# Where a TensorE operand begins inside its SBUF slot: slots with spare bytes, and a shift that depends on the streaming width

## The chip, the cores and the metric

The kernel runs on one core of one Trainium2 chip. The metric is the device time of one execution in microseconds (us); the time before is the median of three executions. Everything below is float32: the large matrix products run on TensorE (PE) in the type float32r, the rest in float32.

## The reference, cut to what matters

One layer of a hybrid decoder over 512 positions of width 2048. The parts that cost time are the matrix products with the weights w_in, w_glu, w_out, w_gate, w_up and w_down.

```python
h = x
hn = _rmsnorm(h, norm1_g)
q, k, v, u = jnp.split(hn @ w_in, [1024, 2048, 3072], axis=-1)
attn_out = _dilated_attention_mixer(q, k, v, cos, sin)      # 8 heads of 128
ssm_out = _s5_mixer(u, ..., w_glu, b_glu)                   # scan over positions, then GELU and a sigmoid gate
h = h + jnp.concatenate([attn_out, ssm_out], axis=-1) @ w_out
hn = _rmsnorm(h, norm2_g)
h = h + (jax.nn.silu(hn @ w_gate) * (hn @ w_up)) @ w_down   # D_FF = 5632
return _rmsnorm(h, final_g)
```

## The kernel before, in words

All activations are kept transposed: the 128 partitions hold features, the free axis holds the 512 positions. A product tile of 128 output features is summed in one PSUM bank over blocks of 128 input features.

**Three products for one.** To keep float32 accuracy with float32r products, every operand is split into a high part and a low part (`split`: ScalarE, ACT, writes the high part, VectorE, DVE, subtracts it and writes the low part). `mm3` then issues three matmuls for each block: line 108 is high weights times high activations, line 109 high weights times low activations, line 110 low weights times high activations. In each, the weights are the stationary operand (128 columns, loaded by a weight load, PEld), the activations the moving operand that is streamed past it, 512 or 256 columns at a time. In the v product (lines 549 to 551) it is the other way round: the activations x are stationary and the weights are streamed.

**The stages** follow each other on PE in this order: u (the state-space input), q, k and v, each 512 columns wide; attention heads; glu; oa (w_out times the attention half, 512 wide); os (w_out times the state-space half, 256 wide, two passes os0 and os1); gate/up, called gu, 256 wide; dn (w_down, 512 wide); and dl, w_down's last group of four row blocks, 256 wide. Gate and up are computed by a Strassen-like scheme of seven half-width products, A to G, for each of 44 feature tiles and each of the two halves of the input features. In the code's order a half runs A, C, B, D, E, F, G, and each product is four blocks of three matmuls, 12 matmuls. A takes its activations from c1, B also from c1, C from c4, D and F from c3, E and G from c2. The main loop has 11 phases; a phase is four gate/up tiles, and behind the first of them the 16 dn tiles of the phase before. The first five tiles get A and B early, while DVE still makes c2, c3 and c4.

**Where operands lie.** Activations that TensorE streams lie in slots of 4096 bytes per partition (`[128, 2, 512]` of four-byte elements: high half, low half; or two operands of two 256-column halves). The slots are in rings: tag A0 and tag A1 (eight each), B in ring2 (eight), a and C in mlp (four each). A slot is used again and again by whatever has its tag: A0 holds x0 to x7, then the attention outputs attn, then c1; A1 holds x8 to x15, then ssm, then c3; B holds ysp, then c2; a holds the gate/up outputs m; C holds c4. Weights lie in five high and five low buffers of 2048 bytes, used in turn by all products. Small `pad` tiles shift the rings. The allocator's addresses in the built program, as the first byte of an operand within its partition modulo 256 (all parts of an operand lie whole multiples of 256 bytes apart, so one number stands for all):

| operand | streamed in | columns | before | changed |
|---|---|---|---|---|
| x0 to x7 / x8 to x15 | u, q, k (stationary in v) | 512 | 64 / 128 | 0 / 0 |
| ysp | glu | 512 | 192 | 16 |
| attn | oa | 512 | 64 | 32 |
| ssm | os | 256 | 128 | 160 |
| c1 (products A, B) | gate/up | 256 | 64 | 192 |
| c2 (E, G) | gate/up | 256 | 192 | 192 |
| c3 (D, F) | gate/up | 256 | 128 | 192 |
| c4 (C) | gate/up | 256 | 64 | 208 |
| m, phases 1 to 10 | dn | 512 | 0 | 0 |
| m, last phase | dl | 256 | 0 | 192 |
| weights whi, wlo (all stages; streamed in v) | stationary | | 0 | 0 |
| weights whi_dl / wlo_dl, in slots B / A0 | stationary in dl | | 192 / 64 | 0 / 0 |

The order of the work is set by a scheduler when the program is built. It is fixed for each engine; semaphores hold an instruction until what it needs is there. SyncE (SP) issues nearly all DMAs in one queue.

Of the kernel before, what the change touches and what calls it, by code (L numbers as in the profile page):

```python
# [11 lines left out]
F32 = mybir.dt.float32  # L12
F32R = mybir.dt.float32r
# [14 lines left out]
NC_ = 64  # L28
RAW = 4
HB = 5  # L30
EPS = 1e-6
SCALE = HD ** -0.5


def _emit(tc, a, y):
    nc = tc.nc
# [124 lines left out]


    ring = opened("ring", bufs=1)
    pad(ring, 64)
    for t in ("A0", "A1"):
        first = ring.tile([128, 2, 512], F32R, tag=t, name="first" + t, bufs=8)
        nc.gpsimd.memset(first[:, 0, 0:2].bitcast(F32), 0.0)
        if t == "A0":
            pad(ring, 64)

    def slot(tag, name):
        return ring.tile([128, 2, 512], F32R, tag=tag, name=name, bufs=8)

    ssacc = cpool.tile([128, 512], F32, tag="ss", name="ssacc")
    rstd = ssacc
# [120 lines left out]
    for n in (1, 2, 4):  # L296
# [4 lines left out]
        t_ = pt[:, :, :n]  # L301
# [231 lines left out]
    mask = vpool.tile([128, 512], F32, name="mask")  # L533
    nc.sync.dma_start(mask, a["mask"])
    ring2 = opened("ring2", bufs=1, side="right")
    first = ring2.tile([128, 2, 512], F32R, tag="B", name="firstB", bufs=8)
    nc.gpsimd.memset(first[:, 0, 0:2].bitcast(F32), 0.0)
    pad(ring2, 800)


    vs = [vpool.tile([128, 1024], F32, name=f"v{m}") for m in range(4)]
# [15 lines left out]
    for b in range(8):  # L557
        yt = wpool.tile([128, 512], F32, tag="sq", name=f"yt{b}", bufs=4)
        nc.sync.dma_start(yt, sy[b].rearrange("p i c -> p (i c)"))
        t_ = ring2.tile([128, 2, 512], F32R, tag="B", name=f"ysp{b}", bufs=8)  # L560
        split(t_[:, 0, :], t_[:, 1, :], yt)
        ysp.append(t_)

# [20 lines left out]
    for h in range(NH):  # L584
        Pb, Tb = nxt
        if h + 1 < NH:
            nxt = scores(h + 1)
        po = acc(f"po{h}")
        for step in "t0 t1 t2 p0 t3 p1 p2 p3".split():
            j = int(step[1])  # L590
            w = 512 - 128 * j
            PT = Tb[j // 2][:, j % 2, :]
            if step[0] == "t":
                tp = acc(f"tp{h}_{j}")
                for i in range(j, 4):
                    pe.transpose(tp[:, 128 * (i - j):128 * (i - j) + 128], Pb[i // 2][:, i % 2, 128 * j:128 * j + 128], ident)
                act.activation(PT[:, :w], tp[:, :w], AF.Copy)
            else:
                pe.matmul(po[:, 128 * j:512], vs[j][:, 128 * h:128 * h + 128], PT[:, :w], start=j == 0, stop=j == 3)
        o = slot("A0", f"attn{h}")  # L600
        act.activation(o[:, 0, :], po, AF.Copy)
        tt(o[:, 1, :], po, o[:, 0, :].bitcast(F32), ALU.subtract)
        attn.append(o)
# [3 lines left out]
    for f in range(8):  # L607
        ps = acc(f"glu{f}")
        ftile(ps, [a["w_glu"][f]], ysp, f"glu{f}")
        g_ = wpool.tile([128, 512], F32, tag="sq", name=f"gate{f}", bufs=4)  # L610
        act.activation(g_, ps, AF.Sigmoid, bias=bg[:, f:f + 1])
        yt = wpool.tile([128, 512], F32, tag="sq", name=f"yr{f}", bufs=4)
        nc.sync.dma_start(yt, sy[f].rearrange("p i c -> p (i c)"))
        z = wpool.tile([128, NC_, T], F32, tag="sq", name=f"gz{f}", bufs=4)
        tt(z.rearrange("p c i -> p i c"), yt.rearrange("p (i c) -> p i c", i=T), g_.rearrange("p (i c) -> p i c", i=T), ALU.mult)
        o = slot("A1", f"ssm{f}")
        split(o[:, 0, :], o[:, 1, :], z.rearrange("p c i -> p (c i)"))
        ssm.append(o)
    closed("v")
# [14 lines left out]
    ss2 = cpool.tile([128, 512], F32, tag="ss", name="ss2")  # L634
    rstd2 = ss2
    mp = opened("mlp", bufs=1)
    pad(mp, 128)
    first = mp.tile([128, 2, 512], F32R, tag="a", name="firsta", bufs=4)
    nc.gpsimd.memset(first[:, 0, 0:2].bitcast(F32), 0.0)
    pad(mp, 64)  # L640

    def comb(tag, name, pool_=None, bufs=8):

        return (pool_ or ring).tile([128, 2, 2, 256], F32R, tag=tag, name=name, bufs=bufs)

    early = {}

# [6 lines left out]
    def split_early(f, hh):  # L654
        raw = load_first(f, hh)
        early[f, hh] = []
        for i in range(2):
            t_ = ring2.tile([128, 2, 512], F32R, tag="B", name=f"w{'AB'[i]}{f}_{hh}", bufs=8)
            split(t_[:, 0], t_[:, 1], raw[:, 512 * i:512 * i + 512])
            early[f, hh].append((t_[:, 0], t_[:, 1]))  # L660

# [5 lines left out]
    c1, c2, c3, c4, n1 = [], [], [], [], []  # L667

    def first_half(k):
        n_ = mp.tile([128, 2, 2, 256], F32, tag="a", name=f"n1_{k}", bufs=4) if k % 2 == 0 else n1[-1][1]  # L670
        n1.append((n_[:, k % 2], n_))
        tc.keep_in_program_order(norm(n1[k][0][:, 0], k, E[0]))
        norm(n1[k][0][:, 1], k + 8, E[0])
# [60 lines left out]
    def gu(f, bank0=None):  # L734
# [28 lines left out]
        tt(u_[:, E[1]], u_[:, E[0]], P[5], ALU.add)  # L763
        tt(u_[:, E[0]], u_[:, E[0]], P[4], ALU.add)
        tt(g_, g_, u_, ALU.mult)
        o = mp.tile([128, 2, 512], F32R, tag="a", name=f"m{f}", bufs=4)
        split(o[:, 0, :], o[:, 1, :], g_)
        return o

    NEARLY = 5  # L770
    first = [gu_first(f) for f in range(NEARLY)]
    for k in range(8):
        es = E[1]
# [16 lines left out]
        c3.append(t3)  # L790

    ssf = cpool.tile([128, 512], F32, tag="ss", name="ssf")
    NPH = 11

    def down(p, ms):
        for c in range(8):
# [20 lines left out]
    for c in range(8):  # L817
        raw = wpool.tile([128, 1024], F32, tag="raw", name=f"raw_dl{c}", bufs=RAW)
        nc.sync.dma_start(raw, a["w_down"][8 * (NPH - 1) + c])
        hi = ring2.tile([128, 2, 512], F32R, tag="B", name=f"whi_dl{c}", bufs=8).rearrange("p a b -> p (a b)")  # L820
        lo = slot("A0", f"wlo_dl{c}").rearrange("p a b -> p (a b)")
        split(hi, lo, raw)
        ws.append((hi, lo))
# [100 lines left out]
```

## Time and profile before

| | |
|---|---|
| time before, median of 3 executions | 2132.87 us (2131.88 to 2133.87) |
| the profiled execution's own time | 2136.28 us |
| its span, first to last instruction | 2134.5 us |
| PE busy | 2078.9 us (97%), 13522 matmul records |
| PEld busy | 1878.8 us (88%) |
| DVE busy | 1539.8 us (72%) |
| ACT busy | 866.4 us (41%) |
| POOL (GpSimd) busy | 198.2 us (9%) |
| chain that ended last | PE 89%, DVE 6%, the rest 5% |

Busy times are shares of the span. Matmuls are pipelined and their ends are modelled in the profile, so a matmul's recorded duration is longer than the time until the next one starts (a 256-column matmul of gate/up is recorded with about 0.28 us). What PE really spends on a matmul is read from the starts of matmuls that follow each other.

### The profile page before, as it was taken

What the parts mean: (1) busy time and instruction counts of PE and PEld (TensorE: products, weight loads), DVE (VectorE), ACT (ScalarE), POOL (GpSimd) and SP (SyncE); (2) the same over time, 40 slices, a digit from 0 to 9 for tenths busy, and PEclk for the clock granted to TensorE, in tenths of its full rate; (3) what the DMA queues carried; (4) which work ended last, traced back from release to release, by engine and by line L of the source; (5) the groups of instructions that cost most, each with busy time, mean ns of one, the idle gap of its engine ahead of it and who ended that gap; (6) DMA issues with size and microseconds to landing.
All of it is one profiled execution on the core that took longest, in us unless ns stands there. A gap on an engine that the chain in (4) does not pass through costs nothing.

```text
span 2134.5 us, 35169 instructions
## 1 busy us (share of the span) xinstructions
PE 2078.9 (97%) x13522; PEld 1878.8 (88%) x13522; DVE 1539.8 (72%) x2932; ACT 866.4 (41%) x1523; POOL 198.2 (9%) x179
## 2 busy tenths in 40 slices
PE   7899999999999979999999999999999999999996
PEld 5688888877889979899998989899998989999896
DVE  7834897546436889686786858687686868778686
ACT  5222222346325645343443525344352535344354
POOL 4433102300002360000000000000000000000001
PEclk9899999999999989999999999999999999999998
DMA  6444334523325614323232333323232332323232
GB/s 219 125 118 114 96 98 138 163 91 124 123 91 170 205 60 139 119 99 119 96 116 87 106 102 110 115 84 129 89 118 81 110 108 100 119 83 126 89 120 79
DMA packets 117193, 244.24 MB, mean 114 GB/s; under 512 B 39040, under 2 KB 57312, under 8 KB 117024
## 3 DMA queue, kind: packets, MB, share of 16 engines
q1 hardware_dynamic: 107808, 239.88, 34.3%
q10 hardware_dynamic: 9216, 2.10, 0.5%
q8 instruction: 106, 1.74, 0.3%
q14 instruction: 63, 0.52, 0.1%
HBM read 229.77 MB, written 9.03 MB: 112 GB/s over the span
## 4 chain that ended last, share of the span: by engine, by line
PE 89%; DVE 6%; issue 2%; DMA 1%; ACT 1%; POOL 0%; SPq 0%; DVEq 0%; ACTq 0%; POOLq 0%
PE gu L108 13%; PE gu L109 13%; PE gu L110 12%; PE dn L109 7%; PE dn L110 7%; PE dn L108 7%; PE q L109 1%; PE q L110 1%; PE lps L436 1%; PE q L108 1%; PE v L549 1%; PE v L551 1%; PE v L550 1%; PE k L109 1%; PE k L108 1%
## 5 line engine op out<-in xcount | busy, mean ns | idle before, releaser
L109 PE MATMUL dn<-m,whi_dn 128*128 128x512 f32 x640 | 249.0, 389 | 0.0
L110 PE MATMUL dn<-m,wlo_dn 128*128 128x512 f32 x640 | 248.8, 389 | 0.0
L108 PE MATMUL dn<-m,whi_dn 128*128 128x512 f32 x640 | 248.8, 389 | 0.0
L49 DVE TENSOR_TENSOR h<-h,dn 128x512 f32<-128x512 f32 x160 | 110.0, 688 | 172.6 <-PE dn L110 171.5
L89 ACT ACTIVATE whi_dn<-raw_dn 128x512 fp32r<-128x512 f32 x160 | 100.9, 632 | 243.3 <-PE dn L109 208.4
L49 DVE TENSOR_TENSOR raw_r<-raw_r,raw_r 128x512 f32<-128x512 f32 x264 | 183.1, 693 | 2.2
L110 PEld LDWEIGHTS dn<-m,wlo_dn 128*128 128x128 f32 x640 | 120.1, 188 | 24.9
L109 PEld LDWEIGHTS dn<-m,whi_dn 128*128 128x128 f32 x640 | 120.1, 188 | 24.6
L108 PEld LDWEIGHTS dn<-m,whi_dn 128*128 128x128 f32 x640 | 120.1, 188 | 24.6
L49 POOL TENSOR_TENSOR h<-h,ssf 128x256 f32<-128x256 f32 x12 | 10.7, 918 | 1317.2 <-ACT ssf L159 1317.2
L49 DVE TENSOR_TENSOR wlo_dn<-raw_dn,whi_dn 128x512 fp32r<-128x512 f32 x160 | 109.8, 687 | 19.7 <-ACT whi_dn L89 18.4
L108 PE MATMUL gu<-c,whi_D 128*128 128x256 f32 x352 | 99.9, 284 | 2.6 <-ACT whi_D L89 2.6
L110 PE MATMUL gu<-c,wlo_E 128*128 128x256 f32 x352 | 98.8, 281 | 2.6 <-DVE wlo_E L49 2.6
L110 PE MATMUL gu<-c,wlo_D 128*128 128x256 f32 x352 | 99.4, 282 | 2.0 <-DVE wlo_D L49 2.0
L108 PE MATMUL gu<-c,whi_E 128*128 128x256 f32 x352 | 98.7, 280 | 2.3 <-ACT whi_G L89 1.7
L108 PE MATMUL gu<-c,whi_C 128*128 128x256 f32 x352 | 98.8, 281 | 1.7 <-ACT c L89 1.6
L109 PE MATMUL gu<-c,whi_D 128*128 128x256 f32 x352 | 99.9, 284 | 0.0
L109 PE MATMUL gu<-c,whi_F 128*128 128x256 f32 x352 | 99.7, 283 | 0.0
L110 PE MATMUL gu<-c,wlo_F 128*128 128x256 f32 x352 | 99.5, 283 | 0.0
L108 PE MATMUL gu<-c,whi_F 128*128 128x256 f32 x352 | 99.4, 282 | 0.0
L109 PE MATMUL gu<-c,whi_C 128*128 128x256 f32 x352 | 98.9, 281 | 0.1
L110 PE MATMUL gu<-c,wlo_C 128*128 128x256 f32 x352 | 98.5, 280 | 0.5 <-DVE wlo_C L49 0.5
(325 smaller groups left out, 6692.1 us busy)
## 6 DMA issues: line engine op xcount, KB each, us to landing
raw_r<-w_gu SPq DMA_DIRECT2D x176, 512.0 KB, 3.5
raw_dn<-w_down SPq DMA_DIRECT2D x80, 512.0 KB, 3.5
raw_os<-w_out SPq DMA_DIRECT2D x32, 512.0 KB, 3.4
raw_q<-w_q SPq DMA_DIRECT2D x16, 512.0 KB, 3.5
raw_k<-w_k SPq DMA_DIRECT2D x16, 512.0 KB, 3.4
raw_v<-w_v SPq DMA_DIRECT2D x16, 512.0 KB, 3.6
raw_oa<-w_out SPq DMA_DIRECT2D x16, 512.0 KB, 3.5
raw_u<-w_u SPq DMA_DIRECT2D x15, 512.0 KB, 4.9
```

The source lines that it names most:

```text
L49: (eng or dve).tensor_tensor(out=out, in0=in0, in1=in1, op=op)
L89: act.activation(hi, raw, AF.Copy)
L108: pe.matmul(ps, wh, x[:, 0, :], start=first, stop=False)
L109: pe.matmul(ps, wh, x[:, 1, :], start=False, stop=False)
L110: pe.matmul(ps, wl, x[:, 0, :], start=False, stop=last)
L436: pe.matmul(lps[:, g, :], tm_[:, :, :, g].rearrange("p i q -> p (i q)"), U[:, 8 * b + g, :], start=True, stop=True)
L549: pe.matmul(pss[m], xs[kt][:, 0, ms], wh, start=kt == 0, stop=False)
L550: pe.matmul(pss[m], xs[kt][:, 0, ms], wl, start=False, stop=False)
L551: pe.matmul(pss[m], xs[kt][:, 1, ms], wh, start=False, stop=kt == 15)
```

## The change

Each slot grows from 1024 to 1088 elements, 4352 bytes or 17 times 256, so all slots of a ring begin at the same address modulo 256. A new helper `laid` takes 1024 elements out of such a slot from a given element on. The shift is chosen where an operand is made: 0, 4 or 8 elements for those streamed 512 columns at a time, 40, 48 or 52 for those streamed 256 at a time (the table above gives the resulting addresses). The pads and the placeholder tiles `first...` of the rings go, with their memsets; ring2 keeps its own, with another pad. Matmuls, splits and their order on PE, ACT and DVE are the same in both programs.

```diff
--- before.py
+++ after.py
@@ -28,6 +28,7 @@
 NC_ = 64
 RAW = 4
 HB = 5
+RPAD = 992
 EPS = 1e-6
 SCALE = HD ** -0.5
 
@@ -161,15 +162,15 @@
 
 
     ring = opened("ring", bufs=1)
-    pad(ring, 64)
-    for t in ("A0", "A1"):
-        first = ring.tile([128, 2, 512], F32R, tag=t, name="first" + t, bufs=8)
-        nc.gpsimd.memset(first[:, 0, 0:2].bitcast(F32), 0.0)
-        if t == "A0":
-            pad(ring, 64)
-
-    def slot(tag, name):
-        return ring.tile([128, 2, 512], F32R, tag=tag, name=name, bufs=8)
+    SLOT = 1088
+
+    def laid(pool_, tag, name, bufs, o):
+
+        t = pool_.tile([128, SLOT], F32R, tag=tag, name=name, bufs=bufs)
+        return t[:, o:o + 1024].rearrange("p (a b) -> p a b", a=2)
+
+    def slot(tag, name, shift=0):
+        return laid(ring, tag, name, 8, shift)
 
     ssacc = cpool.tile([128, 512], F32, tag="ss", name="ssacc")
     rstd = ssacc
@@ -533,9 +534,9 @@
     mask = vpool.tile([128, 512], F32, name="mask")
     nc.sync.dma_start(mask, a["mask"])
     ring2 = opened("ring2", bufs=1, side="right")
-    first = ring2.tile([128, 2, 512], F32R, tag="B", name="firstB", bufs=8)
+    first = laid(ring2, "B", "firstB", 8, 0)
     nc.gpsimd.memset(first[:, 0, 0:2].bitcast(F32), 0.0)
-    pad(ring2, 800)
+    pad(ring2, RPAD)
 
 
     vs = [vpool.tile([128, 1024], F32, name=f"v{m}") for m in range(4)]
@@ -557,7 +558,7 @@
     for b in range(8):
         yt = wpool.tile([128, 512], F32, tag="sq", name=f"yt{b}", bufs=4)
         nc.sync.dma_start(yt, sy[b].rearrange("p i c -> p (i c)"))
-        t_ = ring2.tile([128, 2, 512], F32R, tag="B", name=f"ysp{b}", bufs=8)
+        t_ = laid(ring2, "B", f"ysp{b}", 8, 4)
         split(t_[:, 0, :], t_[:, 1, :], yt)
         ysp.append(t_)
 
@@ -597,7 +598,7 @@
                 act.activation(PT[:, :w], tp[:, :w], AF.Copy)
             else:
                 pe.matmul(po[:, 128 * j:512], vs[j][:, 128 * h:128 * h + 128], PT[:, :w], start=j == 0, stop=j == 3)
-        o = slot("A0", f"attn{h}")
+        o = slot("A0", f"attn{h}", 8)
         act.activation(o[:, 0, :], po, AF.Copy)
         tt(o[:, 1, :], po, o[:, 0, :].bitcast(F32), ALU.subtract)
         attn.append(o)
@@ -613,7 +614,7 @@
         nc.sync.dma_start(yt, sy[f].rearrange("p i c -> p (i c)"))
         z = wpool.tile([128, NC_, T], F32, tag="sq", name=f"gz{f}", bufs=4)
         tt(z.rearrange("p c i -> p i c"), yt.rearrange("p (i c) -> p i c", i=T), g_.rearrange("p (i c) -> p i c", i=T), ALU.mult)
-        o = slot("A1", f"ssm{f}")
+        o = slot("A1", f"ssm{f}", 40)
         split(o[:, 0, :], o[:, 1, :], z.rearrange("p c i -> p (c i)"))
         ssm.append(o)
     closed("v")
@@ -634,14 +635,10 @@
     ss2 = cpool.tile([128, 512], F32, tag="ss", name="ss2")
     rstd2 = ss2
     mp = opened("mlp", bufs=1)
-    pad(mp, 128)
-    first = mp.tile([128, 2, 512], F32R, tag="a", name="firsta", bufs=4)
-    nc.gpsimd.memset(first[:, 0, 0:2].bitcast(F32), 0.0)
-    pad(mp, 64)
 
     def comb(tag, name, pool_=None, bufs=8):
 
-        return (pool_ or ring).tile([128, 2, 2, 256], F32R, tag=tag, name=name, bufs=bufs)
+        return laid(pool_ or ring, tag, name, bufs, 52 if tag == "C" else 48).rearrange("p a (h t) -> p a h t", h=2)
 
     early = {}
 
@@ -655,7 +652,7 @@
         raw = load_first(f, hh)
         early[f, hh] = []
         for i in range(2):
-            t_ = ring2.tile([128, 2, 512], F32R, tag="B", name=f"w{'AB'[i]}{f}_{hh}", bufs=8)
+            t_ = laid(ring2, "B", f"w{'AB'[i]}{f}_{hh}", 8, 0)
             split(t_[:, 0], t_[:, 1], raw[:, 512 * i:512 * i + 512])
             early[f, hh].append((t_[:, 0], t_[:, 1]))
 
@@ -667,7 +664,7 @@
     c1, c2, c3, c4, n1 = [], [], [], [], []
 
     def first_half(k):
-        n_ = mp.tile([128, 2, 2, 256], F32, tag="a", name=f"n1_{k}", bufs=4) if k % 2 == 0 else n1[-1][1]
+        n_ = laid(mp, "a", f"n1_{k}", 4, 0).bitcast(F32).rearrange("p a (h t) -> p a h t", h=2) if k % 2 == 0 else n1[-1][1]
         n1.append((n_[:, k % 2], n_))
         tc.keep_in_program_order(norm(n1[k][0][:, 0], k, E[0]))
         norm(n1[k][0][:, 1], k + 8, E[0])
@@ -763,11 +760,12 @@
         tt(u_[:, E[1]], u_[:, E[0]], P[5], ALU.add)
         tt(u_[:, E[0]], u_[:, E[0]], P[4], ALU.add)
         tt(g_, g_, u_, ALU.mult)
-        o = mp.tile([128, 2, 512], F32R, tag="a", name=f"m{f}", bufs=4)
+        o = laid(mp, "a", f"m{f}", 4, 48 * (f >= 4 * (NPH - 1)))
         split(o[:, 0, :], o[:, 1, :], g_)
         return o
 
     NEARLY = 5
+    NPH = 11
     first = [gu_first(f) for f in range(NEARLY)]
     for k in range(8):
         es = E[1]
@@ -790,7 +788,6 @@
         c3.append(t3)
 
     ssf = cpool.tile([128, 512], F32, tag="ss", name="ssf")
-    NPH = 11
 
     def down(p, ms):
         for c in range(8):
@@ -817,7 +814,7 @@
     for c in range(8):
         raw = wpool.tile([128, 1024], F32, tag="raw", name=f"raw_dl{c}", bufs=RAW)
         nc.sync.dma_start(raw, a["w_down"][8 * (NPH - 1) + c])
-        hi = ring2.tile([128, 2, 512], F32R, tag="B", name=f"whi_dl{c}", bufs=8).rearrange("p a b -> p (a b)")
+        hi = laid(ring2, "B", f"whi_dl{c}", 8, 0).rearrange("p a b -> p (a b)")
         lo = slot("A0", f"wlo_dl{c}").rearrange("p a b -> p (a b)")
         split(hi, lo, raw)
         ws.append((hi, lo))
```

In the order of the instructions two places differ. On SP the load of `mask` (the attention mask, `[128, 512]`) stood before, between loads for the state-space output (cc, c_c), ahead of the last w_q loads (raw_q):

```order
L94 DMA raw_q_1_2479<-w_q 128x1024
L504 DMA cc_3140<-c_c 128x256
L504 DMA cc_3252<-c_c 128x256
L534 DMA mask<-mask 128x512
L504 DMA cc_3287<-c_c 128x256
L470 DMA sw_q_2284<-qh_2282 16x512
L471 DMA sw_q_2284<-qh_2282 16x512
```

In the changed program it stands among the loads of w_v (raw_v) for the second half of v; behind it come two more of these and the reloads of the state-space output (yt from sy):

```order
L95 DMA raw_v_2_3936<-w_v 128x1024
L95 DMA raw_v_3_3970<-w_v 128x1024
L535 DMA mask<-mask 128x512
L95 DMA raw_v_4_4004<-w_v 128x1024
L95 DMA raw_v_5_4038<-w_v 128x1024
L560 DMA yt_4164<-sy_3452 128x512
```

The load has moved from the middle of the q stage to the v stage. There it waits for the last matmul of the state-space output (yps) and for GpSimd, since its new place overlaps a buffer that they used.

On POOL the start of the program before held the memsets of the pads (line 67) and placeholders (line 167), ahead of the running sum of squares ssacc:

```order
L67 MEMSET pad_58 128x1
L67 MEMSET pad_78 128x1
L167 MEMSET firstA_80 128x2
L67 MEMSET pad_82 128x1
L167 MEMSET firstA_84 128x2
L49 ISA
L49 TENSOR_TENSOR ssacc<-ssacc,sq_x_295 128x512
```

In the changed program one pad is left there:

```order
L917 UNCONDITIONAL_BRANCH
L68 MEMSET pad_58 128x1
L50 ISA
L50 TENSOR_TENSOR ssacc<-ssacc,sq_x_287 128x512
L50 TENSOR_TENSOR ssacc<-ssacc,sq_x_290 128x512
```

Four memsets are gone here, and three more later on.

## Rows read from the trace of the kernel before

**Rows 1.** Busy time by stretch: us, each engine's busy us, PEclk, DMA share, GB/s.

```profile
220.00:370.00 150.00, 150.00 (x676) 123.24 (x676) 129.77 (x393) 35.81 (x57) 17.70 (x12) 1.00 0.36 112
...
692.00:741.00 49.00, 47.76 (x390) 46.58 (x390) 46.12 (x86) 32.34 (x64) 16.97 (x15) 1.00 0.60 199
...
772.00:865.00 93.00, 80.99 (x604) 77.39 (x604) 88.99 (x154) 45.59 (x80) 18.21 (x16) 0.91 0.35 115
865.00:2062.00 1197.00, 1197.00 (x8431) 1122.09 (x8431) 894.05 (x1526) 499.11 (x820) 0.00 (x0) 1.00 0.31 104
2062.00:2134.50 72.50, 53.59 (x442) 51.75 (x440) 51.36 (x114) 33.81 (x77) 10.65 (x12) 0.89 0.28 95
```

**Rows 2.** PE by time, one half of a gate/up tile: start us, recorded us, instruction.

```profile
1671.10 0.28 PE L108 MATMUL gu<-c,whi_A 128*128 128x256 f32 x1
...
1676.76 0.28 PE L108 MATMUL gu<-c,whi_E 128*128 128x256 f32 x1
...
1678.12 0.28 PE L108 MATMUL gu<-c,whi_F 128*128 128x256 f32 x1
...
1679.55 0.28 PE L108 MATMUL gu<-c,whi_G 128*128 128x256 f32 x1
...
1680.93 0.28 PE L108 MATMUL gu<-c,whi_A 128*128 128x256 f32 x1
```

**Rows 3.** Costliest groups of the page, dn: count, busy us, mean ns, idle before.

```profile
L109 PE MATMUL dn<-m,whi_dn 128*128 128x512 f32 x640 | 249.0, 389 | 0.0
```

**Rows 4.** PE by time, one dn tile and the next one's first matmul.

```profile
1364.57 0.39 PE L108 MATMUL dn<-m,whi_dn 128*128 128x512 f32 x1
...
1367.29 0.39 PE L108 MATMUL dn<-m,whi_dn 128*128 128x512 f32 x1
```

**Rows 5.** PE by time, first matmuls of two k tiles that follow each other.

```profile
309.58 0.39 PE L108 MATMUL k<-x,whi_k 128*128 128x512 f32 x1
...
320.65 0.39 PE L108 MATMUL k<-x,whi_k 128*128 128x512 f32 x1
```

**Rows 6.** PE by time, first matmuls of two chunks of v (24 matmuls, x0 to x7).

```profile
436.39 0.40 PE L549 MATMUL v<-whi_v,x 128*128 128x512 f32 x1
...
441.99 0.40 PE L549 MATMUL v<-whi_v,x 128*128 128x512 f32 x1
```

**Rows 7.** PE by time, first matmuls of two glu tiles.

```profile
530.09 0.39 PE L108 MATMUL glu<-ysp,whi_glu 128*128 128x512 f32 x1
...
535.69 0.39 PE L108 MATMUL glu<-ysp,whi_glu 128*128 128x512 f32 x1
```

**Rows 8.** PE by time, first matmuls of two oa tiles.

```profile
585.56 0.39 PE L108 MATMUL oa<-attn,whi_oa 128*128 128x512 f32 x1
...
591.05 0.39 PE L108 MATMUL oa<-attn,whi_oa 128*128 128x512 f32 x1
```

**Rows 9.** PE by time, first matmuls of two os0 tiles.

```profile
660.38 0.28 PE L108 MATMUL os<-ssm,whi_os 128*128 128x256 f32 x1
...
663.26 0.28 PE L108 MATMUL os<-ssm,whi_os 128*128 128x256 f32 x1
```

**Rows 10.** PE by time, 15 dl matmuls.

```profile
2097.22 0.28 PE L108 MATMUL dl<-m,whi_dl 128*128 128x256 f32 x1
...
2099.00 0.28 PE L108 MATMUL dl<-m,whi_dl 128*128 128x256 f32 x1
```

**Rows 11.** PE by time, 12 dl matmuls later on.

```profile
2104.36 0.28 PE L109 MATMUL dl<-m,whi_dl 128*128 128x256 f32 x1
...
2105.72 0.28 PE L109 MATMUL dl<-m,whi_dl 128*128 128x256 f32 x1
```

**Rows 12.** Busy time in a stretch of four gate/up tiles, columns as in rows 1.

```profile
1030.70:1109.50 78.80, 78.80 (x674) 78.79 (x673) 65.50 (x114) 39.76 (x67) 0.00 (x0) 1.00 0.34 114
```

**Rows 13.** Instructions that read the mask: count, ns, first and last start.

```profile
L575 DVE CUSTOM_DVE_ANT_0 P<-sc,mask x32: 280/480/693, 450.6 to 505.3; 128x128 f32<-128x128 f32 x8, 128x256 f32<-128x256 f32 x8, 128x384 f32<-128x384 f32 x8, 128x512 f32<-128x512 f32 x8
```

**Rows 14.** SP by time: the raw_v loads before, and the yt behind them.

```profile
397.90 25.16 SPq L94 DMA_DIRECT2D raw_v<-w_v  x6
423.60 2.13 SPq L559 DMA_DIRECT2D yt<-sy  x4
```

## The prediction

> **What bounds the kernel now.** I read the busy times by stretch first, to find where PE sets the time, then PE's starts inside each stage. From 865 to 2062 us, the regular main loop and 56% of the span, PE is busy all 1197.0 us, with the clock at its upper level (PEclk 1.00, 2.4 GHz), and DVE for 894 us [rows 1]. No wait ends there on another engine, so the time is the number of matmuls times the distance between their starts. Of the 8431 matmuls in it 1920 are dn (three lines of 640), with no idle time before them [rows 3].
>
> A start-to-start distance is the reading that matters. A dn tile of 12 matmuls takes 1367.29 - 1364.57 = 2.72 us, 226.7 ns each [rows 4]. In gate/up, products of the same shape differ: E takes 1678.12 - 1676.76 = 1.36 us for 12, 113.3 ns each; F 1.43 us, 119.2 ns; G 1.38 us, 115 ns; A, C, B and D together 5.66 us for 48, 117.9 ns [rows 2]. The whole half takes 9.83 us for 84, 117.0 ns on average. The stretch agrees: (1197.0 - 1920 x 0.2267) / 6511 = 117.0 ns. E and F have the same weights' buffers in turn, the same shape, no wait; what tells them apart is where the moving operand lies: E's at 192 modulo 256, F's at 128.
>
> Is it the address of the moving operand, or its distance from that of the stationary one? I call (moving - stationary) modulo 256 the **distance**. With 512 columns:
>
> - dn: 0 - 0, distance 0: 226.7 ns [rows 4]
> - oa: 64 - 0, distance 64: 5.49 us for 24, 228.8 ns [rows 8]
> - k: half its matmuls at 64, half at 128: 11.07 us for 48, 230.6 ns [rows 5], so 2 x 230.6 - 228.8 = 232.4 ns at 128
> - glu: 192 - 0, distance 192: 5.60 us for 24, 233.3 ns [rows 7]
> - v: moving weights at 0, stationary x at 64, distance 192: 5.60 us, 233.3 ns [rows 6]
>
> v streams from 0 just as dn does and is not as fast; it has glu's distance and glu's pace. So I read the distance as the cause. With 256 columns: distance 192 is 113.3 ns (E), 128 is 119.2 (F) and 120.0 in os (2.88 us for 24) [rows 2, 9], and 64 is near 117.9 (A, B, C are three of the four products in that sum). dl mixes distances 64, 64 and 192 and runs at two paces: 1.78 us for 15, 118.7 ns, and later 1.36 us for 12, 113.3 ns, with the same distances [rows 10, 11]. So a pace can also be handed on from matmul to matmul. E, behind D at 128, is at 113.3 ns on average at once: 192 draws the stream to the short pace.
>
> **What the change does to each stage.** No matmul, split or DMA of weights is added, removed or reordered on PE, ACT and DVE. Distances become 192 for A, B, D, E, F, G and dl, 208 for C, 160 for os, and 0 for x in u, q, k and (as stationary operand) v; 16 for glu, 32 for oa; dn stays at 0.
>
> - Gate/up in the main loop: 6511 x (117.0 - 113.3) = 24.1 us. I take C at 208 like E's 192, the nearest row, only 16 bytes off; if its 936 matmuls (39 tiles of 24) gained nothing, 4.3 us of this would go.
> - q and k: in the stretch from 220 to 370 us PE is busy throughout with 676 records, 628 of them q and k (three yps groups of 16 are the rest) [rows 1]. 628 x (230.6 - 226.7) = 2.4 us.
> - v: 192 matmuls at 233.3, and 192 at distance 128, for which I take k's 232.4; all to 226.7: 1.3 + 1.1 = 2.4 us.
> - glu: distance 16 lies between 0 (226.7) and 64 (228.8); in proportion 227.2. 192 x 6.1 = 1.2 us, at least 0.9 by the end at 64.
> - oa: 32 is midway, 227.8: 384 x 1.0 = 0.4 us, between 0 and 0.8.
> - os: 160 is midway between 128 (120.0) and 192 (113.3), 116.7. os0: 384 x 3.3 = 1.3 us, between 0 and 2.6. os1: nothing, since there DVE is busy 46.1 of 49.0 us [rows 1]; at most 2.6.
> - From 741 to 865 us nothing: from 772 on DVE, which makes c2, c3 and c4, is busy 89.0 of 93.0 us and PE 81.0, so PE would wait longer. At most 1.5 us (the last three tiles, some 350 matmuls at 117 to 113.3, 1.3 us).
> - dl: a saving of 5.4 ns for the part of 384 matmuls at the longer pace; PE is busy 53.6 of 72.5 us in the tail, with DVE and the last DMAs on the path. I take 0.5 us, between 0 and 1.5.
> - u: nothing, at most 1 us.
> - The mask load: 512 columns, moved past the q, k and first v loads on SP. It now waits for yps, and two raw_v loads and the yt reloads wait behind it. Before, that place of the queue was passed by 423.6 us [rows 14]; the mask is first read at 450.6 us [rows 13]. That leaves 27 us; cost 0. If that cover went, the first scores would wait for it and PE for them, microsecond for microsecond.
> - The seven memsets on POOL: one column or two each, ahead of sums that POOL takes up only when x has arrived; 0.
>
> Sum: 24.1 + 2.4 + 2.4 + 1.2 + 0.4 + 1.3 + 0.5 = 32.3 us. From the profiled execution's 2136.28 us (1.8 us more than its span) that gives 2104.0 us. It stands 3.4 us above the median, so the median becomes 2132.9 - 32.3 = 2100.6, say **2101 us**. With every upper end (oa 0.8, os 5.2, the 1.5 before 865, dl 1.5, u 1.0) the gain is 40 us, 2093. With every lower end (C nothing, os, oa and dl nothing, glu 0.9) it is 25.5 us, 2107.
>
> What hides nothing else: DVE has 65.5 us of recorded work in four gate/up tiles of 78.8 us [rows 12], and these would take 672 x 113.3 = 76.1 us.
>
> A rule that speaks against all this: the Trainium skill (TensorE: Matmul & The Clock Gate, Part 2) gives PE two independent read ports, so that loading the next weights takes no read bandwidth from the running matmul. By it the distance between the two operands cannot matter, and v, dn and glu should run alike; the kernel would stay at 2133. The rows on v and on E against F disagree.
>
> **The rivals.**
>
> 1. *Starts off a multiple of 64 bytes cost.* All streams of the rows lie at multiples of 64; 16, 32, 160 and 208 don't. Bounded by the worst rows (120.0 ns at 256 columns, 233.3 at 512): C at 120.0 costs 936 x 6.7 = 6.3 us against the sum, os gains nothing (1.3), oa loses 384 x 5.5 = 2.1, glu gains nothing (1.2). That is 10.9 us less gain, 2112. For it: no row excludes it. Against it: the paces at 64 and at 128 differ by little. The Trainium skill (SBUF — State Buffer, Specifications) speaks of 16-byte lines; all four starts are multiples of 16, so by that page there is no such cost, and no run here shows it yet.
> 2. *DVE or the split weights come late.* PE is faster by 3%, and gate/up waits for wlo. If half the gain of gate/up is lost, 2113. Against it: 65.5 of 76.1 us [rows 12], and PE never waits in the main loop before.
> 3. *The slot's address is not the cause.* E would be fast for another reason (its weights' place in the order), and nothing moves: 2133, no change. Against it: v, and G, which also reads c2 and starts at 115 ns although F runs ahead of it. (It is the case that the two ports of the Trainium skill's TensorE page, cited above, would give.)
> 4. *Slower: the longer pace is held.* The dl rows show one set of distances at 113.3 and at 118.7. If the whole gate/up stream, now all at 192 and 208, held os's 120.0 ns, the main loop would lose 6511 x 3.0 = 19.5 us against 8.2 us gained elsewhere: 2144. It decides from 117.0 + 8.2 / 6511 = 118.3 ns on. Against it: E falls to 113.3 in every half shown, whatever ran before it.
>
> **How the numbers follow.** My forecast, 0.76: 2093 to 2107, likeliest 2101. Rival 1: 0.10, rival 2: 0.05, rival 3: 0.05, rival 4: 0.04. A change under 0.2% (4.3 us) can't be told from none; only rival 3 lies within it, rivals 1 and 2 are still faster by 0.9%. So faster 0.91, same 0.05, slower 0.04. The range takes in the forecast and most of rival 1: 2092 to 2112.
>
> **What would show it.** In the changed kernel's trace each of the seven products of a half should take 1.36 us from its first start to the next one's, a half 9.52 us; a v chunk 5.44 us; a k tile 10.88 us; dn stays at 2.72. C at 1.41 or more, os at 2.88 or glu at 5.60 per tile would show the starts that no row covers to be worth nothing. PE idle before wlo in gate/up would be rival 2, a half at 9.8 us rival 3, at 10 us or more rival 4. The forecast fails if the pace depends on something that the rows hold constant, such as the slot's place in units larger than 256 bytes.

## The result and the profile after

The changed kernel takes 2115.9 us, median of 4 executions (2112.28 to 2117.73), against 2133.4 (2131.88 to 2134.78) for the kernel before in the same comparison: ratio 0.9913, 95% interval 0.9899 to 0.9927, 17.5 us less. It is faster by 0.9%, little more than half of the 32.3 us forecast, and its time lies above the range of the forecast.

The profiled executions are 24.0 us apart (2136.28 and 2112.28), more than the medians: each kernel's executions scatter. The four of the changed kernel, from the fastest to the slowest, ran at a mean granted clock of 0.986, 0.985, 0.983 and 0.983. Part of it shows in the two traces. Up to the third u tile (45.8 us before, 43.5 after) TensorE's mean granted clock is 0.89 before and 0.92 after, between the two levels of 1.2 and 2.4 GHz, and that part alone makes 2.3 us; in a second profile of the unaltered changed kernel (after_again, below) it takes 45.2 us, so most of this is not the change's. From the k stage on the traces can be compared stage by stage.

Busy time by stretch of the changed kernel, columns as in [rows 1]: the main loop, and the tail.

```profile
857.60:2037.70 1180.10, 1180.10 (x8432) 1105.31 (x8431) 890.57 (x1525) 499.13 (x820) 0.00 (x0) 1.00 0.31 106
2037.70:2110.50 72.80, 53.47 (x442) 51.65 (x441) 51.60 (x115) 33.87 (x77) 10.67 (x12) 0.89 0.28 95
```

The main loop has as many matmuls as before, PE is busy without a break at the upper clock, and it takes 1180.1 us where [rows 1] have 1197.0: 16.9 us less. The tail takes as long as before, to 0.3 us. So the gain is made of start-to-start distances, as forecast, and the shortfall has to lie there too.

PE by time, changed kernel: first matmuls of the seven products of one half, and of the next half's A.

```profile
1652.61 0.28 PE L109 MATMUL gu<-c,whi_A 128*128 128x256 f32 x1
...
1653.97 0.28 PE L109 MATMUL gu<-c,whi_C 128*128 128x256 f32 x1
...
1655.39 0.28 PE L109 MATMUL gu<-c,whi_B 128*128 128x256 f32 x1
...
1656.77 0.28 PE L109 MATMUL gu<-c,whi_D 128*128 128x256 f32 x1
...
1658.13 0.28 PE L109 MATMUL gu<-c,whi_E 128*128 128x256 f32 x1
...
1659.49 0.28 PE L109 MATMUL gu<-c,whi_F 128*128 128x256 f32 x1
...
1660.85 0.28 PE L109 MATMUL gu<-c,whi_G 128*128 128x256 f32 x1
...
1662.21 0.28 PE L109 MATMUL gu<-c,whi_A 128*128 128x256 f32 x1
```

A, D, E, F and G take the 1.36 us forecast (113.3 ns a matmul). C, at distance 208, takes 1.42 us (118.3), and B behind it 1.38: its first four matmuls still go at C's pace. The half takes 9.60 us; 9.83 before [rows 2], 9.52 forecast. In the first half behind dn, A is held up as well. PE by time there:

```profile
1623.73 0.28 PE L109 MATMUL gu<-c,whi_A 128*128 128x256 f32 x1
...
1625.15 0.28 PE L109 MATMUL gu<-c,whi_C 128*128 128x256 f32 x1
...
1626.57 0.28 PE L109 MATMUL gu<-c,whi_B 128*128 128x256 f32 x1
```

A takes 1.42 us here, at distance 192, where it takes 1.36 in the other seven halves of a phase. One distance, two paces.

The trace of before had this too. PE by time, kernel before: first matmuls of E and F in a half behind dn.

```profile
1769.44 0.28 PE L108 MATMUL gu<-c,whi_E 128*128 128x256 f32 x1
...
1770.82 0.28 PE L108 MATMUL gu<-c,whi_F 128*128 128x256 f32 x1
```

E takes 1.38 us here (115.4 ns) for the 1.36 of [rows 2], in every regular phase. And over a phase D runs at 117.9 ns and F at 119.0, both at distance 128.

PE by time in the stages whose distances no row of before covered, and in v: two first matmuls each.

```profile
431.73 0.39 PE L550 MATMUL v<-whi_v,x 128*128 128x512 f32 x1
...
437.17 0.39 PE L550 MATMUL v<-whi_v,x 128*128 128x512 f32 x1
...
538.39 0.39 PE L109 MATMUL glu<-ysp,whi_glu 128*128 128x512 f32 x1
...
543.96 0.39 PE L109 MATMUL glu<-ysp,whi_glu 128*128 128x512 f32 x1
...
560.71 0.39 PE L109 MATMUL oa<-attn,whi_oa 128*128 128x512 f32 x1
...
566.31 0.39 PE L109 MATMUL oa<-attn,whi_oa 128*128 128x512 f32 x1
...
650.63 0.28 PE L109 MATMUL os<-ssm,whi_os 128*128 128x256 f32 x1
...
653.51 0.28 PE L109 MATMUL os<-ssm,whi_os 128*128 128x256 f32 x1
```

v, at distance 0, takes 5.44 us for 24 matmuls, 5.60 before [rows 6]. glu at 16 takes 5.57, hardly less than 5.60 [rows 7]. oa at 32 takes 5.60, more than the 5.49 before [rows 8]. os at 160 takes 2.88, as before [rows 9].

### The profile page after: what moved, and what is told of

The parts are those of the page before. It is cut to its first block, busy times and chain, and to the rows that moved or that the text cites. A ratio compares the mean times of both kernels' runs of the same rounds, so it can differ in the third digit from the quotient of the medians.

```text
span 2110.5 us, 35164 instructions
## 1 busy us (share of the span) xinstructions
PE 2053.3 (97%) x13522; PEld 1858.4 (88%) x13522; DVE 1535.6 (73%) x2932; ACT 865.6 (41%) x1523; POOL 198.1 (9%) x172
## 4 chain that ended last, share of the span: by engine, by line
PE 87%; DVE 7%; issue 2%; DMA 1%; ACT 1%; SPq 0%; POOL 0%; DVEq 0%; ACTq 0%; POOLq 0%
PE gu L109 12%; PE gu L111 12%; PE gu L110 12%; PE dn L110 7%; PE dn L109 7%; PE dn L111 7%; PE lps L437 1%; PE q L111 1%; PE q L110 1%; PE oa L111 1%; PE oa L109 1%; PE oa L110 1%; PE q L109 1%; PE v L550 1%; PE v L552 1%
## 5 line engine op out<-in xcount | busy, mean ns | idle before, releaser
L109 PE MATMUL gu<-c,whi_E 128*128 128x256 f32 x352 | 98.5, 280 | 2.4 <-ACT whi_G L90 1.7
L110 PE MATMUL gu<-c,whi_E 128*128 128x256 f32 x352 | 98.3, 279 | 0.0
L109 PE MATMUL gu<-c,whi_F 128*128 128x256 f32 x352 | 97.7, 277 | 0.0
L109 PE MATMUL gu<-c,whi_G 128*128 128x256 f32 x352 | 97.5, 277 | 0.2 <-ACT whi_G L90 0.2
```

The lines of the kernel that those rows point to most:

```text
L109: pe.matmul(ps, wh, x[:, 0, :], start=first, stop=False)
L110: pe.matmul(ps, wh, x[:, 1, :], start=False, stop=False)
```

## The experiments

All later kernels are told with one number that hardly scatters: the time from the first dn matmul of one phase to that of the next. In each trace it is the same in all eight regular phases. A phase has 192 dn and 672 gate/up matmuls; the forecast asks for 192 x 0.2267 + 672 x 0.1133 = 119.7 us. PE by time, first dn matmuls of two phases, in the changed kernel and then in all64, a kernel told of below:

```profile
1459.76 0.39 PE L109 MATMUL dn<-m,whi_dn 128*128 128x512 f32 x1
...
1580.20 0.39 PE L109 MATMUL dn<-m,whi_dn 128*128 128x512 f32 x1
```

```profile
1461.35 0.39 PE L109 MATMUL dn<-m,whi_dn 128*128 128x512 f32 x1
...
1581.79 0.39 PE L109 MATMUL dn<-m,whi_dn 128*128 128x512 f32 x1
```

Whole executions of one kernel scatter by 3 to 10 us, and most of these kernels were timed once, so the phase carries the argument and the execution only agrees with it.

| kernel | distance of C / of the other six | phase, us | execution(s), us |
|---|---|---|---|
| before | 64 / 64, 128, 192 | 122.19 | 2133.4 |
| changed | 208 / 192 | 120.44 | 2115.9 |
| all64 | 208 / 192, all 64 bytes further on | 120.44 | 2116.07 |
| grid | 208 / 192 | 120.44 | 2110.39 |
| c192 | 192 / 192 | 122.67 | 2134.93 |
| kick | 192 / 192, and 12 extra matmuls at 208 | 121.19 | 2127.71 |
| c112 | 112 / 192 | 120.35 | 2113.18 |
| all112 | 112 / 112 | 119.75 | 2105.2, median of 4 |
| shift0 | 0 / 0 | 124.18 | 2155.09 |

**Pace against distance, by itself.** A small kernel streams copies of x, 96 matmuls at a time, with the layer's pattern of three matmuls per block and a weight load each; only the moving operand's start changes.

```python
for i in range(16):
    seg.append((f"{c}{LET[i]}", N, 16 * i, 0))     # name, columns, moving start, stationary start
...
for i in range(4):
    seg.append((f"w{LET[i]}s", 512, 64 * i, 64))   # the stationary start 64 bytes further on
```

> This kernel computes no part of the layer: it streams 96 float32r matmuls (three for each of 32 blocks, as in mm3) for each distance between moving and stationary start, 0 to 240 bytes in steps of 16, at 256 and 512 columns, in two orders, then with the stationary side 64 bytes further, then in steps of 4. Theory distance: at 64, 128, 192 and 0 the paces of the kernel come back (256 columns: 118, 119 to 120, 113.3; 512: 228.8, 232.4, 233.3, 226.7), with the stationary side 64 further they move along by 64, and 208, 160 at 256 columns and 16, 32 at 512 show what the changed kernel shows (208 near 118.7, oa's 32 above 229). Rival absolute start: with the stationary side 64 further each moving start keeps its pace. Rival place in the kernel (other engines' accesses, neighbouring products): all distances run alike here.

PE by time, this kernel. The first letter of a name is the width (n 256, w 512 columns), the second the moving start (a 0, b 16, c 32, h 112, k 160, m 192, n 208, p 240); s is the stationary start at 64, y a second pass in another order. Start us, time of the whole group us, instruction; the pace is that time less its last matmul's recorded 0.28 (0.39 at 512 columns) by 95.

```profile
40.09 11.68 PE L65 MATMUL na<-M,W 128*128 128x256 f32 x96
...
119.90 11.04 PE L65 MATMUL nh<-M,W 128*128 128x256 f32 x96
...
153.56 11.43 PE L65 MATMUL nk<-M,W 128*128 128x256 f32 x96
...
176.27 11.05 PE L65 MATMUL nm<-M,W 128*128 128x256 f32 x96
187.16 11.60 PE L65 MATMUL nn<-M,W 128*128 128x256 f32 x96
...
221.22 21.96 PE L65 MATMUL wa<-M,W 128*128 128x512 f32 x96
243.02 22.40 PE L65 MATMUL wb<-M,W 128*128 128x512 f32 x96
265.25 22.57 PE L65 MATMUL wc<-M,W 128*128 128x512 f32 x96
...
555.50 21.93 PE L65 MATMUL wp<-M,W 128*128 128x512 f32 x96
...
777.84 22.86 PE L65 MATMUL wpy<-M,W 128*128 128x512 f32 x96
...
1013.70 11.47 PE L65 MATMUL nmy<-M,W 128*128 128x256 f32 x96
...
1161.01 22.56 PE L65 MATMUL was<-M,W 128*128 128x512 f32 x96
1183.40 21.94 PE L65 MATMUL wbs<-M,W 128*128 128x512 f32 x96
```

At 256 columns 0 gives 120.0 ns, 112 gives 113.3, 160 117.4, 208 119.2. 192 gives 113.4 the first time and 117.8 the second: it has two paces. Of the 16 multiples of 16 only 112 was short both times (113.3 and 113.7, the last half of each group at 113.3); all others but 192 lie between 116.7 and 120. At 512 columns 0 gives 227.1, 16 231.7, 32 233.5; 64, 128 and 192 give 229.1, 232.4 and 233.4, the paces that the prediction read in oa, k and glu. 192 is not the only start with more than one pace: at 512 columns 240 gives 226.7 and then 236.5, at 256 columns 16 and 144 give about 118.7 and then 116.7, and 160, here at 117.4 and 117.3, is at 120.0 in the changed kernel's os0. With the stationary operand moved by 64 the short pace moves along: moving start 0 gives 233.4, and 64 gives 226.8. So the distance counts, but the pace is not smooth in it: 16 bytes away from a good distance lies a bad one.

**C at 192 like the others.** If only C's 208 was bad, this should have brought the missing 7 us.

```diff
-... 52 if tag == "C" else 48)
+... 48)
```

> Only c4's shift is 48 elements in place of 52, so product C is at distance 192 like the other six. Theory offset (208 itself is a long-pace distance and B pays for what C leaves behind): C falls from 118.7 to 113.4 ns, B from 115.3 and A from 114.2 to 113.5; the gate/up stretch of the main loop gets 936 x 5.3 + 936 x 1.8 + 936 x 0.7 = 7.3 us shorter, the execution about 7 us. Rival ring (c4 lies in the mlp pool, and C runs between two products on c1): C stays near 118 and the time within 1 us.

It took 2134.93 us in one execution, beside 2135.51 for the kernel before on the same chip: the gain of gate/up was gone. PE by time, first matmuls of E and F, and of F and G:

```profile
1663.90 0.28 PE L109 MATMUL gu<-c,whi_E 128*128 128x256 f32 x1
...
1665.32 0.28 PE L109 MATMUL gu<-c,whi_F 128*128 128x256 f32 x1
...
1666.73 0.28 PE L109 MATMUL gu<-c,whi_G 128*128 128x256 f32 x1
```

E at 192 takes 1.42 us and F 1.41; all seven products stay near 117.8 ns, in every half. Nothing breaks the longer pace within a phase, it is handed on from product to product, and behind each dn it is there again. Both expectations fell. The new theory: 192 has two paces, and which one a stream takes is settled when it enters that distance; it then keeps it. Then C's 208, bad itself, was what let B and all behind it fall to 113.3 in the changed kernel.

**Everything 64 bytes further on**, weights too, so that addresses change and distances don't.

```diff
-RPAD = 992
+RPAD = 928
-    pad(cpool, 480)
+    pad(cpool, 544)
```

> The changed kernel with every float32r operand, moving and stationary, 64 bytes further: all distances stay, all addresses modulo 256 move by 64 (x and m at 64, c1 to c3 at 0, c4 at 16). Theory distance: every stage keeps its pace, time within 3 us of the changed kernel. Rival absolute start: dn goes from 226.7 to about 228.8 ns (1920 x 2.1 = 4 us) and six gate/up products take the unknown pace of start 0 instead of 113.4, anything up to 120, at which the main loop is some 35 us longer.

2116.07 us; the phase is the same to 0.01 us, and k and v are within 0.5 ns a matmul. With both operands moved by 64 bytes nothing changes, so the pace goes by the distance and not by an operand's own address.

**attn and ysp at 0, ssm at 192**, gate/up as in the changed kernel.

```diff
-        t_ = laid(ring2, "B", f"ysp{b}", 8, 4)
+        t_ = laid(ring2, "B", f"ysp{b}", 8, 0)
-        o = slot("A0", f"attn{h}", 8)
+        o = slot("A0", f"attn{h}", 0)
-        o = slot("A1", f"ssm{f}", 40)
+        o = slot("A1", f"ssm{f}", 48)
```

> Only attn and ysp at 0 and ssm at 192, C left at 208. Theory offset: oa falls from 234 to 226.7 ns (384 x 7 = 2.8 us), glu to 226.7 (about 1 us), os0 from 120 to 113.4 (2.5 us), os1 something up to that: 6 to 9 us in all. Rival: os is held by its weights' DMA or by DVE; then os gives nothing and 3 to 4 us are left.

2110.39 us in one execution. From glu to the end of os0 the stages take 44.5 + 87.0 + 45.2 us, against 45.4 + 89.6 + 46.1 in the changed kernel: 4.3 us, so the shifts of 4, 8 and 40 elements cost that much. That is less than the 6 to 9 us expected, since os at 192 ran at 117.8 here, the longer of its two paces.

**How the stream enters.** A second small kernel runs 24 matmuls at one distance and then 48 at another.

```python
for e in range(16):
    seg.append((f"{t}{LET[e]}e", 256, 16 * e, 0, 1))   # entry
    seg.append((f"{t}{LET[e]}t", 256, off, 0, 2))      # 48 at off: 192 (t is m), 112 (t is h)
...
```

> No part of the layer: 24 float32r matmuls at each of 16 entry distances (and 24 at 512 columns, distance 0, as dn ends), each followed by 48 at a target: 192 and then 112 at 256 columns; then, at 512 columns, 0 behind each of the 16; at the end 96 to 128 in steps of 4. Theory history: at 192 some entries lead to 113.3 ns and others to 117.8 for all 48, the one behind 512 columns at 0 to 117.8; a distance that holds one pace only shows it behind every entry (112 may be one: 113.3 both times so far; 0 at 512 columns: 226.7). Rival fixed pace: 192 shows one pace behind every entry once some matmuls have passed.

PE by time: groups at 192 behind entries at 0, 16, 64, 208, and behind 512 columns at 0 (as after dn); then a group at 116.

```profile
41.95 5.62 PE L62 MATMUL mat<-M,W 128*128 128x256 f32 x48
...
50.21 5.82 PE L62 MATMUL mbt<-M,W 128*128 128x256 f32 x48
...
75.25 5.61 PE L62 MATMUL met<-M,W 128*128 128x256 f32 x48
...
150.25 5.61 PE L62 MATMUL mnt<-M,W 128*128 128x256 f32 x48
...
177.72 5.82 PE L62 MATMUL mwt<-M,W 128*128 128x256 f32 x48
...
619.45 6.00 PE L62 MATMUL ffz<-M,W 128*128 128x256 f32 x48
```

The pace is the time less 0.28 by 47: 113.6 behind 0, 117.9 behind 16, 113.4 behind 64 and 208, 117.9 behind dn's width. Behind 12 of the 16 entries 192 went at the short pace, behind 16, 128, 144 and 160 and behind 512 columns at the long one, for all 48. 112 ended at 113.3 behind all 17 entries, behind some only after 13 matmuls. 116, one element on, is at 121.7. At 512 columns, distance 0 ended at 226.7 behind all 16. So a stream of nothing but matmuls shows both what A does behind dn and what c192 did throughout. The distance of the entry does not decide by itself, though: behind 64 the group at 192 is short here, and in the first small kernel, where 192 followed 64 in the second order (nmy), it was long.

**C alone at 112, and all of 256 columns at 112** (attn and ysp at 0).

```diff
-... 52 if tag == "C" else 48)
+... 28 if tag == "C" else 48)      # c112
+... 28)                            # all112, and the same for ssm and the last m
```

> Only C moves, from 208 to 112; the other six stay at 192. Theory history: C itself runs at 113.3 (112 showed nothing else); whether B, D, E, F and G then take 113.3 or 117.8 depends on how C hands over, so the main loop is either some 7 us shorter than the changed kernel's (about 2107) or some 20 us longer (about 2133). Rival fixed pace at 192 of 113.3, with C's ring at fault in both earlier kernels: C stays near 118.

> All operands streamed 256 columns at a time at distance 112 (c1 to c4, ssm, the last m), all streamed 512 at 0 (x, ysp, attn). Theory history, if 112 and 0 each hold one pace: all seven products 113.3 ns, os0 113.3, oa, glu, v 226.7; against the changed kernel C gives 936 x 5.4, B 936 x 1.8, A 936 x 0.6 (7.3 us), os0 2.6, os1 up to 2, oa 2.5, glu 0.9: 13 to 15 us, so about 2102 by the median. Rival: 112 also has a longer pace in the real stream; then gate/up is at 117 or more and the time near 2125 to 2135.

c112 took 2113.18 us in one execution, and C stayed at 119.1 ns: behind A at the short pace only the last of its 12 matmuls takes 113 ns. In the small kernel too 112 settles only after 11 matmuls when it follows 192. B behind it was better, 113.9 ns for 115.1. all112 took 2105.2 us, median of 4 (2099.83 to 2106.47): ratio to the kernel before 0.9856, interval 0.9835 to 0.9878, the fastest kernel of the study. Every product is at 113.3 but A behind dn, which is at 116.6 while it settles. PE by time there, A and C of another half:

```profile
1649.32 0.28 PE L109 MATMUL gu<-c,whi_A 128*128 128x256 f32 x1
...
1650.68 0.28 PE L109 MATMUL gu<-c,whi_C 128*128 128x256 f32 x1
```

**The changed kernel again**, on the chip of all112.

> The changed kernel unaltered, timed on the same chip beside all112: 2112 to 2118 as before, with C at 118.7 and B at 115.1 ns in every phase.

2116.49 us (2113.85 to 2118.48), ratio 0.9917, interval 0.9899 to 0.9934, and the same phase. The result stands.

**Work added to c192.** Behind the first A of each phase, 12 more matmuls at distance 208, into a bank whose sum starts anew later.

```diff
+                if hh == 0 and f % 4 == 1:
+                    for k in range(4):
...
+                        off = raw4[k][:, 52:564].rearrange("p (a t) -> p a t", a=2)
+                        mm3(banks[3][:, E[0]], wA[0][:, sl], wA[1][:, sl], off, k == 0, k == 3)
...
```

> c192 (all seven products at 192, all at 117.8 ns) with 12 extra matmuls, ten times in the main loop: behind the first A after each dn, A's weights times c4 read 16 bytes further on (distance 208), into C's PSUM region before C overwrites it. Their result is not used. Theory history: these 12 do what product C at 208 does in the changed kernel, so that C, B, D, E, F and G of that half and all products up to the next dn run at 113.3; the main loop from gu5 to dl0 falls from c192's 1157.9 us to 1129.5 + 10 x 1.43 + 10 x 0.1 = 1145 us although 120 matmuls are added. Rival (some property of the slots in c192 holds 117.8): the loop grows by 14.3 us to 1172.

This is the sharpest test of the theory of entry, and it held: from the first gate/up matmul behind phase 0's dn to the first of dl it takes 1144.1 us, c192 1157.9, with 120 matmuls more; 1145 was expected. (The executions, on different chips, are 2127.71 and 2134.93 us.) Twelve extra matmuls at 192 were not tried, but in c192 C itself is twelve at 192, and nothing falls behind it. PE by time, from the A behind dn on:

```profile
1636.15 0.28 PE L109 MATMUL gu<-c,whi_A 128*128 128x256 f32 x1
...
1638.99 0.28 PE L109 MATMUL gu<-c,whi_C 128*128 128x256 f32 x1
...
1640.37 0.28 PE L109 MATMUL gu<-c,whi_B 128*128 128x256 f32 x1
1641.73 0.28 PE L109 MATMUL gu<-c,whi_D 128*128 128x256 f32 x1
```

A and the 12 extra take 2.84 us, 118.3 a matmul. C then settles within its 12 (1.38 us), and B and all others take 1.36 us until the next dn. The phase falls from 122.67 to 121.19, of which the extra matmuls are 1.42: without them it would be 119.77, and all112 has 119.75.

**Slots alone**, all shifts 0, so that every stage is at distance 0.

> The slots of 4352 bytes alone, all shifts 0: every distance is 0. Theory: at 512 columns 226.7 ns everywhere (u, q, k, v, glu, oa: 7 us less than before), at 256 columns 120 ns, which is all that distance 0 showed: gate/up 6511 x (120.0 - 117.0) = 19.5 us more than before, os0 as before. About 2146. Rival (the spare bytes themselves help, whatever the shift): faster than before.

2155.09 us in one execution, 21.5 more than the kernel before on that chip; about 2146 was expected. The phase is 1.99 us longer than before, and from the profiled executions the main loop is 19.3, near the 19.5 expected; where the other 9 us lie was not followed. Streams of 512 columns go at 226.7 to 227.3 ns in q, k, v, glu, oa and dn, but those of 256 at 119.8 to 120.0, os and the seven products alike. Without a shift by width the slots lose.

**Fewer columns of weights**, the first test of a cause: if reads of the weights collide with those of the stream, fewer of them should cost less.

```python
for t, cols in (("h", 64), ("q", 32), ("f", 128)):
    for e in range(16):
        seg.append((f"{t}{LET[e]}c", 256, 16 * e, 0, 2, cols))
```

> No part of the layer: 48 float32r matmuls of 256 columns at each of the 16 distances, with 64, with 32 and with 128 stationary columns. Theory collision (the reads of the next weight load and of the stream delay each other): with 64 and 32 columns the weight load reads half and a quarter of the bytes, and what a distance costs above 113.3 ns shrinks with it, to a quarter or so at 32. Rival stream alone (each start costs by itself): the paces of 128 columns come back at 64 and 32.

PE by time: distance 16 with 64 columns of weights, 112 with 64, 16 with 32, 16 with 128.

```profile
45.53 5.77 PE L54 MATMUL hbc<-M,W 128*64 128x256 f32 x48
...
79.34 5.77 PE L54 MATMUL hhc<-M,W 128*64 128x256 f32 x48
...
135.28 5.62 PE L54 MATMUL qbc<-M,W 128*32 128x256 f32 x48
...
223.84 5.87 PE L54 MATMUL fbc<-M,W 128*128 128x256 f32 x48
```

118.9 ns with 128 columns, 116.8 with 64, 113.6 with 32. Over all 16 distances the last 24 matmuls lie on average 4.6, 3.5 and 1.4 ns above 113.3, and 14, 14 and 6 of the 16 are above 114. Less weight, less excess on average, though not in proportion. But it isn't so for each distance: with 64 columns 112 is at 116.8 (113.3 with 128) and 192 at 118.7 (113.6), while 0 falls from 119.8 to 113.4. So the width of the weights also changes which distances are short, and the reading for 112 holds for 128 columns. This fits a collision of weight loads with the stream; it does not show that, nor where they would meet, since a matmul with fewer columns of weights also writes fewer rows of its result, and each width ran in one order only, while some distances have more than one pace.

## Why the prediction was wrong

The direction was right, and so was the distance as the cause. Wrong was how the pace follows from the distance: it was taken to be smooth in it and to be one value for each. By stage, from the two profiled executions (us gained; forecast 32.3 in sum):

| term | forecast | measured | why |
|---|---|---|---|
| gate/up, main loop | 24.1 | 16.9 | C 118.7 ns, B 115.1, A 113.9 on average, D to G 113.3 |
| q, k | 2.4 | 2.8 | 227.0 ns, forecast 226.7; the forecast counted 628 of 768 matmuls |
| v | 2.4 | 2.0 | 227.3 ns |
| glu | 1.2 | 0.3 | 231.7 ns at 16, forecast 227.2 |
| oa | 0.4 | -1.7 | 233.3 ns at 32, forecast 227.8 |
| os0 | 1.3 | 0.0 | 120.0 ns at 160, forecast 116.7 |
| os1, 741 to 865 us | 0 | 0.5 | DVE sets the time, as said |
| dl | 0.5 | -0.3 | within the scatter of one execution |
| u, up to its third tile | 0 | 2.3 | mostly the granted clock, see above |
| u, the rest | 0 | 1.1 | 230.9 to 227.8 ns; clock 0.92 and 0.94 |

The measured terms add up to 23.9, the two spans differ by 24.0. The medians gained 17.5; the further 6.5 is the scatter of single executions (before, 2.9 above its median; after, 3.6 below). Without u, the stages gained 20.5 of the 32.3: 7.2 are missing in gate/up, 4.3 in glu, oa and os0, 0.8 in dl and 0.4 in v, while q, k and os1 gave 0.9 more. By the medians another 3.0 are missing, and no trace shows where. That u would give nothing was stated without a reason; its matmuls became 3 ns shorter, since x is streamed there too.

**The step that failed** is "I take C at 208 like E's 192, the nearest row, only 16 bytes off". C lost 5.4 ns on 936 matmuls, 5.1 us; B behind it 1.8, 1.7 us; A behind dn 0.6, 0.6 us. Together 7.4 us, where 7.2 were missing in gate/up. The lower end allowed for C gaining nothing (4.3) but not for its getting worse (117.8 before, 118.7 after) or for its neighbours. The three values taken "in proportion" or "midway" for 16, 32 and 160 failed in the same way, 0.9, 2.1 and 1.3 us: four points 64 bytes apart were read as a smooth curve, and the sweep shows there is none. oa and glu even left their stated bounds (0 to 0.8, and at least 0.9).

**A sentence that fell with it** is "192 draws the stream to the short pace". It was read from E, which follows D at 128 and is short in [rows 2]; but 192 holds either pace, as c192, kick and the entries showed. The ground given against rival 4, that E falls to 113.3 "whatever ran before it", rested on one half; behind dn E was at 115.4 in the same trace. One step further, C at 192, the prediction's own logic would have forecast its 24 us and met a loss of 4.6 us in the main loop (1157.9 us from the first gate/up matmul behind phase 0's dn to the first of dl, against 1153.3 before). So that gate/up gained at all was in part luck: the one shift taken to be a small risk, C's 208, is what brought the other six to the short pace.

**The rivals.** Rival 1 had the size nearly right (2112, measured 2115.9; C, glu, os and oa nearly as it says), but not the reason: 112, which is no multiple of 64, is the best distance at 256 columns, and 0, 64 and 128 are poor ones. Rival 2 is out, PE has no break in the main loop. Rival 3 is out: all64 kept every pace while all addresses moved, and the distances alone (shift0, c192, all112) moved the phase from 119.75 to 124.18. Its ground, the two independent read ports of the Trainium skill (TensorE: Matmul & The Clock Gate, Part 2), doesn't agree with these runs, if it is taken to mean that the two operands cannot hinder each other: at equal shapes the distance between them moves a matmul from 113.3 to 121.7 ns, and fewer weight columns lessen the mean excess. The measurement decides. Rival 4, the longer pace held, did not come in this kernel but in c192, at 117.8 ns, one shift away; at 0.04 it was priced too low for what [rows 10, 11] had shown, two paces with the same distances.

**Right**: the reading of distance rather than address; D to G and dn to 0.1 ns, q, k and v to 0.6; os1 at nothing (in all112 os0 falls to 113.4 ns and os1 still takes 49.9 us, 49.3 before), and the stretch up to 865 us within its bound; the mask load and the memsets at nothing. all112 reached 2105.2 us, 29.9 below the kernel before on its chip, and 2.44 us a phase of the 2.49 forecast: the gain in gate/up was there, at another shift.

**Open.** Why 112 settles at the short pace wherever it was tried with 128 columns of weights, and what decides the pace at 192: E behind D at 128 fell to the short pace before, while 192 behind an entry at 128 held the long one in the small kernel, and behind 64 it did either. Slots lie 4096 bytes apart before and 4352 in all other kernels here, and no run tested whether the distance modulo 256 says all of it. In the changed kernel's slower executions, which left no trace, the place of the 2 to 5 us isn't known.

## What to carry to other kernels

Where PE never waits, read its start-to-start distances product by product: equal shapes at unequal paces are worth a look at where both operands begin. Don't interpolate between starts; measure each at the real width, behind the real neighbours, and prefer one that falls to the short pace whatever ran before (here, with 128 columns of weights, a distance of 0 at 512 columns and 112 at 256). When an operand looks merely slow, ask what it does to those behind it before moving it: making C equal to its neighbours cost 2.2 us a phase.

## What the runs showed of the hardware that was not expected

- The pace of a float32r matmul with its weight load depends on the distance of the two operands' starts down to single elements: at 256 columns 113.3 ns at 112, 121.7 at 116; at 512 columns 226.7 at 0, 238.2 at 4, 231.1 at 252 and 240 at 244 (further groups of the first two small kernels). The Trainium skill (SBUF — State Buffer, Specifications) gives lines of 16 bytes; 112 and 116 begin in the same line, so lines alone don't order these paces.
- One distance can hold two paces for as long as nothing disturbs it: 192 at 256 columns, 113.3 or 117.8 ns, the latter for all 672 matmuls between two dn in c192; and 240 at 512 columns, 226.7 or 236.5 ns, each for a whole group of 96.
- Twelve useless matmuls a phase made the main loop 13.8 us shorter (kick against c192).
